# Transposing the merged branch sum in 32x32 blocks on VectorE instead of on TensorE

## The chip, the cores and the metric

The kernel runs on one core of a Trainium2 chip. The metric is the device time of one execution in microseconds (us). The kernel before takes 2072.56 us, the median of 3 runs (2072.18 to 2073.11).

## The reference, cut to what matters

Two layers are computed for 256 tokens of width 2048, all in float32. Three branches (sparse attention, convolution, stick-breaking attention) give gated activations of width 1024. Each is projected to 2048 features, and the three projections are merged by sigmoid gates. One output projection of the merged sum is added to the layer's input:

```python
y_a = (dsa_attention(...) * silu(za)) @ w_a_out
y_b = (conformer_conv(...) * silu(zb)) @ w_b_out
y_c = (stick_breaking_attention(...) * silu(zc)) @ w_c_out
g = sigmoid(gates).reshape(b, s, N_BRANCH, D_MODEL)
merged = g[:, :, 0] * y_a + g[:, :, 1] * y_b + g[:, :, 2] * y_c
return x + merged @ w_out
```

After the second layer comes a last RMSNorm. The change concerns `merged`, between the gates and `w_out`.

## The kernel before, in words

**Units.** Weights are read from HBM in units of 512 KB, 128 partitions x 1024 float32 numbers, and the whole kernel is a row of such units. To multiply float32 numbers accurately, each weight and each activation is split into a high part in the type fp32r and a low remainder. `load_unit` (L181) has SyncE issue the DMA into `raw`; `high` (L202, the copy at L204) has ScalarE (ACT) round it into `wh`; `low` (L206, the subtraction at L208) has VectorE (DVE) form `wl = raw - wh`. `raw` has four buffers, `wh` and `wl` have three each. So `wh` of a unit can be written only when TensorE (PE) is done with the `wh` of the unit three before it, and a `raw` is loaded only when DVE has read the one four before it.

**Products.** `chunk_N` (L277) computes 512 output features for 256 tokens, tokens on the partitions. Each unit is 12 matmuls of 512 columns (`token_products`, L268): four with the activations' high part and `wh`, four with their low part and `wh`, four with their high part and `wl`. PE waits for `wh` at the unit's start and for `wl` at its last third. The activations are the stationary operand, so they have to lie with features on the partitions.

**The merge (L829 to L860).** For each branch b in the order 0, 2, 1 and each quarter j of the 2048 features there is a gate chunk (8 units of `w_in`), a sigmoid by ACT (L849), a projection chunk (4 units of `w_a`, `w_c` or `w_b`), and a product and sum by DVE (L855, or L857 and L858) into `mg`, tokens on the partitions. In the last pass, b = 1, `mg` is complete for quarter j after each projection chunk. It is then turned by `turn(j)` (L819), so that features lie on the partitions, and split into a high and a low part, `mx` (`split_at`, which ends in ACT's copy at L311 and DVE's subtraction at L312).

**The old turn.** It is a generator that `start` puts on a list; `background`, called after each unit's matmuls, resumes it one unit later. Eight PE transposes (L824) of 128x128 write the PSUM tile `mm`; ACT and DVE then split it, at raised priority, straight from PSUM.

**What follows.** Four chunks with `w_out` (L906 to L936) read `mx`, eight units of two 128-feature blocks each. Units 6 and 7 of the first of them are the first to read the last quarter of `mx`, the one that `turn(3)` makes. `residual` (L877) loads the layer's input into a `t4` tile for the add at L889, and for the last layer L871 loads the final norm's weights.

**Order.** The order on each engine and on SyncE's DMA queue is set by a scheduler that ranks instructions by their place in the program, raised where the code says `tc.high_priority()`, and that lets an instruction stand only where its buffer would be free by the scheduler's own reckoning. `t4` is a pool of four buffers of 128 x 1024; it serves the residual tiles, the convolution's norm and the attention branches.

Of the kernel before, what the change touches and what calls it, by code (L numbers as in the profile page):

```python
# [14 lines left out]
P = 128  # L15
S = 256
NT = S // P
# [31 lines left out]
def trunk(ctx: ExitStack, tc: tile.TileContext, x, w_in, w_a, w_b, w_c, w_out,  # L49
          fnw, consts, out):  # L50
    nc = tc.nc
# [25 lines left out]
    ident = cst[:, C_ID:C_ID + P]  # L77
# [15 lines left out]
    def nm(s):  # L93
        uid[0] += 1
        return f"{s}_{uid[0]}"
# [4 lines left out]
    def big():  # L100
        return [slot(), slot()]
# [4 lines left out]
    def parts(n, own=()):  # L106
        own = list(own)
        return own + [slot(F32R).rearrange("p (k w) t -> p k w t", w=2) for _ in range(n // 4 - len(own))]
# [4 lines left out]
    def hi(b, k, n=1, ts=slice(0, S)):  # L113
        return part(b, 0, k, n, ts)

    def lo(b, k, n=1, ts=slice(0, S)):
        return part(b, 1, k, n, ts)

    def split_at(b, k, n, src, ts=slice(0, S)):
        split(hi(b, k, n, ts), lo(b, k, n, ts), src)  # L120

    def mm_tile():
        return mp.tile([P, 1024], F32, tag="mm", name=nm("mm"))
# [4 lines left out]
    def t4():  # L128
        return tp.tile([P, 1024], F32, tag="t4", bufs=4, name=nm("t4"))

    def ev():
        return tp.tile([P, 512], F32, tag="ev", bufs=3, name=nm("ev"))
# [21 lines left out]
    def start(gen):  # L154
        stages.append([gen, 0])

    def finish():
        while stages:
            advance(stages[0])
# [14 lines left out]
    def flush():  # L174
        while waiting:
            for f in waiting.pop(0)[1]:
                f()
# [43 lines left out]
    def chunk_T(w, c0, n, act, nk, t0=0):  # L221
        acc = acc_tile()
        nf = n // P
        nt = S - t0
        ku = min(8, 1024 // n)
        for k0 in range(0, nk, ku):
            wh, wl = unit(w, k0, ku, [(c0, n)])
            for k in range(ku):
                both = act[(k0 + k) // 4][:, (k0 + k) % 4, :, t0:]
                for f in range(nf):  # L230
                    mult(acc[:, f, :2 * nt].rearrange("p (w t) -> p w t", w=2), wh[:, k, f * P:(f + 1) * P],
                         both, k0 + k == 0, False)
            for k in range(ku):
                for f in range(nf):
                    mm = mult(acc[:, f, :nt], wl[:, k, f * P:(f + 1) * P], hi(act, k0 + k)[:, 0, t0:],
                              False, k0 + k == nk - 1)
            background(mm)
        return acc[:, :nf, :2 * nt]
# [7 lines left out]
    def summed(acc):  # L246
        nf = acc.shape[1]
        v = ev()[:, :nf * acc.shape[2] // 2]
        v3 = v.rearrange("p (f t) -> p f t", f=nf)
        total(acc, v3)  # L250
        return v, v3
# [25 lines left out]
    def chunk_N(w, segs, act, nk, ku=2):  # L277
        acc = acc_tile()
        n = sum(c for _, c in segs)
        accs = [acc[:, t, :] for t in range(NT)]  # L280
        for k0 in range(0, nk, ku):
            background(token_products(accs, n, unit(w, k0, ku, segs), act, k0, ku, nk, range(NT)))
        return accs
# [26 lines left out]
    def split(h, l, src):  # L310
        nc.scalar.copy(h, src)  # L311
        nc.vector.tensor_sub(l, src, h.bitcast(F32))  # L312
# [31 lines left out]
    def gate(c0, o, b, w, hx):  # L344
        for k in range(0, KC, 2):
            a, a3 = summed(chunk_T(w, c0 + k * P, 256, hx, KD))
            sg = sigmoid_of(a)
            with tc.high_priority():
                nc.vector.tensor_mul(a3, a3, sg)
                nc.vector.tensor_mul(a3, a3, o[:, k:k + 2, :])  # L350
                split_at(b, k, 2, a3)
# [47 lines left out]
    for layer in range(DEPTH):  # L399
# [153 lines left out]
        for j in range(2):  # L553
            for i in range(2):
# [5 lines left out]
                else:  # L560
                    sg = sigmoid_of(summed(chunk_T(w, O_UG + c0 * P, 256, hx, KD))[0])
                    a = summed(chunk_T(w, O_UA + c0 * P, 256, hx, KD))[1]
# [29 lines left out]
        a = chunk_N(w, [(O_VA, 256), (O_WI, NIH)], hx, KD)  # L592
# [129 lines left out]
        for j in range(2):  # L722
            a = chunk_N(w, [(O_VC + j * 512, 512)], hx, KD)
# [59 lines left out]
        def conv_norm(cv=cv, pr=pr):  # L783
            work = t4()
            red = [work[:, i * S:(i + 1) * S] for i in range(4)]
            sums = red[2:]
            for i in range(2):
                nc.vector.tensor_reduce(red[i], cv[:, i * 4:i * 4 + 4, :].rearrange("p c t -> p t c"), op=ALU.add, axis=AX.X)
            nc.vector.tensor_add(red[0], red[0], red[1])
            yield 3  # L790
            ps = mm_tile()
            nc.tensor.matmul(ps[:, :S], mean_w, red[0], start=True, stop=True)
            for i in range(2):
                cs = cv[:, i * 4:i * 4 + 4, :]
                nc.vector.tensor_sub(cs, cs, heads(ps[:, :S], 4))
                sq = t4()
                nc.scalar.activation(sq.rearrange("p (c t) -> p c t", c=4), cs, AF.Square)
                nc.vector.tensor_reduce(sums[i], sq.rearrange("p (c t) -> p t c", c=4), op=ALU.add, axis=AX.X)
            nc.vector.tensor_add(sums[0], sums[0], sums[1])
            yield 6  # L800
            vs = mm_tile()
            nc.tensor.matmul(vs[:, :S], mean_w, sums[0], start=True, stop=True)
            r = rsqrt_mean(vs[:, :S], 1, t4())
            for i in range(2):
                cs = cv[:, i * 4:i * 4 + 4, :]
                nc.vector.tensor_mul(cs, cs, heads(r, 4))
                sg = t4()
                for c in range(4):
                    cc = i * 4 + c
                    lw, lb = pr[:, P_LW + cc:P_LW + cc + 1], pr[:, P_LB + cc:P_LB + cc + 1]  # L810
                    nc.scalar.activation(sg[:, c * S:(c + 1) * S], cs[:, c, :], AF.Sigmoid, bias=lb, scale=lw)
                    nc.vector.tensor_scalar(cs[:, c, :], cs[:, c, :], lw, lb, op0=ALU.mult, op1=ALU.add)
                nc.vector.tensor_mul(cs, cs, sg.rearrange("p (c t) -> p c t", c=4))
# [3 lines left out]
        mg = [v.rearrange("p a b -> p (a b)").rearrange("p (j t d) -> p j t d", j=2, t=NT) for v in big()]  # L817

        def turn(j, mg=mg):  # L819
            yield 1  # L820
            ps = mm_tile().rearrange("p (k t) -> p k t", t=S)
            for kk in range(4):
                for t in range(NT):
                    nc.tensor.transpose(ps[:, kk, t * P:(t + 1) * P], mg[j // 2][:, j % 2, t, kk * P:(kk + 1) * P],  # L824
                                        ident)
            with tc.high_priority():
                split_at(mx, j * 4, 4, ps)

        for b in (0, 2, 1):  # L829
            if b == 2:  # L830
                finish()
                gc = parts(KC)
                gate(O_ZC, qcT, gc, w, hx)
            if b == 1:
                finish()
                gb = parts(KC)
                gate(O_ZB, cv, gb, w, hx)
                mx = parts(KD)
            gx = ga if b == 0 else gc if b == 2 else gb
            for j in range(4):  # L840
                if b == 2 and j == 1:
                    finish()
                    flush()
                    start(conv_norm())
                g = chunk_N(w, [(O_G + b * D + j * 512, 512)], hx, KD)
                sg = [ev() for _ in range(NT)]
                with tc.high_priority():
                    for t in range(NT):
                        nc.scalar.activation(sg[t], g[t], AF.Sigmoid)  # L849
                y = chunk_N((w_a, w_b, w_c)[b][layer], [(j * 512, 512)], gx, KC)  # L850
                with tc.high_priority():
                    for t in range(NT):
                        dst = mg[j // 2][:, j % 2, t, :]
                        if b == 0:
                            nc.vector.tensor_mul(dst, y[t], sg[t])  # L855
                        else:
                            nc.vector.tensor_mul(sg[t], y[t], sg[t])  # L857
                            nc.vector.tensor_add(dst, dst, sg[t])  # L858
                if b == 1:
                    start(turn(j))  # L860


        last = layer == DEPTH - 1
# [42 lines left out]
        for q in range(3 if last else 4):  # L906
            c0 = q * 512
            tail = residual(c0, 512)
            a = chunk_N(w_out[layer], [(c0, 512)], mx, KD)
# [6 lines left out]
        a = chunk_N(w_out[layer], [(c0, n)], mx, KD, ku=4)  # L916
# [71 lines left out]
```

## Time and profile before

| | |
|---|---|
| median of 3 runs | 2072.56 us (2072.18 to 2073.11) |
| the profiled execution: its own time | 2072.41 us |
| its span, first to last instruction | 2070.6 us |
| outside the span | 1.8 us |
| granted TensorE clock | 0.999 |
| PE busy | 2056.9 us (99%) |
| DVE busy | 1490.4 us (72%) |
| ACT busy | 1067.4 us (52%) |
| DMA | 394.27 MB, mean 190 GB/s |

In the rows that follow, a line number such as L208 is the line of the kernel before. A timeline row gives the start in the span, the time that its merged instructions take, the engine, the line, the operation, output<-input, shapes, how many instructions were merged, and in brackets the engine's idle time before it and what released it. PEld is the load of the stationary operand, which normally runs beside the matmul before it. A grouped row ends in the count, then busy time and mean length of one in ns, then the idle time before the group.

### The profile page before, as it was taken

What the parts mean: (1) busy time and instruction counts of PE and PEld (TensorE: products, weight loads), DVE (VectorE), ACT (ScalarE), POOL (GpSimd) and SP (SyncE); (2) the same over time, 40 slices, a digit from 0 to 9 for tenths busy, and PEclk for the clock granted to TensorE, in tenths of its full rate; (3) what the DMA queues carried; (4) which work ended last, traced back from release to release, by engine and by line L of the source; (5) the groups of instructions that cost most, each with busy time, mean ns of one, the idle gap of its engine ahead of it and who ended that gap; (6) DMA issues with size and microseconds to landing.
All of it is one profiled execution on the core that took longest, in us unless ns stands there. A gap on an engine that the chain in (4) does not pass through costs nothing.

```text
span 2070.6 us, 28574 instructions
## 1 busy us (share of the span) xinstructions
PE 2056.9 (99%) x11056; PEld 1793.6 (87%) x11056; DVE 1490.4 (72%) x2037; ACT 1067.4 (52%) x1309; POOL 0.2 (0%) x4
## 2 busy tenths in 40 slices
PE   9999999999999999999999999999999999999998
PEld 8899888888888888888899998888888888888887
DVE  7678998688776856555576799976887757565555
ACT  6465555466444544444454655554664445444443
POOL 0000000000000000000000000000000000000000
PEclk9999999999999999999999999999999999999999
DMA  7677575665666666666666774756656667666664
GB/s 247 194 220 214 145 204 157 182 179 165 180 190 189 217 209 192 187 190 194 206 191 194 224 204 145 203 152 187 182 162 183 190 194 223 193 192 190 206 196 145
DMA packets 290984, 394.27 MB, mean 190 GB/s; under 512 B 16544, under 2 KB 181536, under 8 KB 290720
## 3 DMA queue, kind: packets, MB, share of 16 engines
q1 hardware_dynamic: 289760, 390.35, 63.6%
q8 instruction: 86, 1.41, 0.3%
q10 hardware_dynamic: 1088, 2.10, 0.3%
q14 instruction: 50, 0.41, 0.1%
HBM read 388.20 MB, written 4.19 MB: 190 GB/s over the span
## 4 chain that ended last, share of the span: by engine, by line
PE 99%; DMA 0%; DVE 0%; ACT 0%; issue 0%; ACTq 0%; SPq 0%
PE acc L218 95%; PE mm L653 1%; PE mm L684 1%; PE mm L373 0%; PE mm L709 0%; PE mm L824 0%; PE mm L772 0%; PE mm L736 0%; PE mm L701 0%; PE mm L758 0%; PE mm L624 0%; PE mm L739 0%; PE mm L774 0%; DMA x<-in_x_dram 0%; PE mm L760 0%; PE mm L763 0%
## 5 line engine op out<-in xcount | busy, mean ns | idle before, releaser
L208 DVE TENSOR_TENSOR wl<-raw,wh 128x1024 fp32r<-128x1024 f32 (+2 forms) x729 | 880.1, 1210 | 474.7 <-ACT wh L204 472.1
L204 ACT CAST wh<-raw 128x1024 fp32r<-128x1024 f32 (+2 forms) x728 | 757.5, 1042 | 848.1 <-PE acc L218 666.5
L218 PE MATMUL acc<-wh,s 128*128 128x512 f32 (+2 forms) x3200 | 775.5, 384 | 0.0
L218 PEld LDWEIGHTS acc<-wh,s 128*128 128x128 f32 x3200 | 587.0, 188 | 114.7
L218 PE MATMUL acc<-s,wh 128*128 128x512 f32 (+2 forms) x2912 | 645.1, 365 | 0.6 <-ACT s L382 0.6
L218 PEld LDWEIGHTS acc<-s,wh 128*128 128x128 f32 x2912 | 492.6, 190 | 62.7 <-ACT s L382 1.0
L218 PE MATMUL acc<-wl,s 128*128 128x512 f32 (+2 forms) x1600 | 417.4, 383 | 0.0
L218 PEld LDWEIGHTS acc<-s,wl 128*128 128x128 f32 x2656 | 356.6, 191 | 18.4
L218 PE MATMUL acc<-s,wl 128*128 128x256 f32 (+1 forms) x2656 | 365.1, 280 | 0.0
L218 PEld LDWEIGHTS acc<-wl,s 128*128 128x128 f32 x1600 | 295.6, 188 | 58.8
L359 DVE SCALAR_TENSOR_TENSOR s<-yT,cst,s 128x256 f32<-128x256 f32 x480 | 217.5, 478 | 0.4
L244 DVE TENSOR_TENSOR ev<-acc,ev 128x512 f32<-128x512 f32 (+2 forms) x60 | 38.4, 640 | 0.0
L857 DVE TENSOR_TENSOR ev<-acc,ev 128x512 f32<-128x512 f32 x32 | 22.0, 688 | 19.3 <-PE acc L218 19.3
L311 ACT CAST s<-ev 128x512 fp32r<-128x512 f32 (+1 forms) x40 | 21.3, 533 | 26.3 <-DVE ev L332 24.5
L325 DVE TENSOR_TENSOR ev<-ev,cst 128x384 f32<-128x384 f32 (+2 forms) x28 | 16.7, 595 | 23.9 <-ACT ev L323 23.8
L243 ACT COPY ev<-acc 128x512 f32<-128x512 f32 (+2 forms) x60 | 32.8, 546 | 0.4 <-PE acc L218 0.4
L312 DVE TENSOR_TENSOR s<-ev,s 128x512 fp32r<-128x512 f32 (+1 forms) x40 | 23.2, 581 | 6.8 <-ACT s L311 6.6
L322 ACT COPY ev<-ev 64x384 f32<-64x384 f32 (+2 forms) x28 | 15.2, 542 | 24.7 <-DVE ev L244 24.3
L849 ACT ACTIVATE ev<-acc 128x512 f32<-128x512 f32 x48 | 26.6, 591 | 0.1
L889 DVE TENSOR_TENSOR t<-acc,t 128x512 f32<-128x512 f32 (+1 forms) x18 | 10.6, 628 | 17.2 <-PE acc L218 17.2
L858 DVE TENSOR_TENSOR s<-s,ev 128x512 f32<-128x512 f32 x32 | 21.9, 685 | 0.0
L341 ACT ACTIVATE ev<-ev 128x512 f32<-128x512 f32 x28 | 17.6, 627 | 0.0
(173 smaller groups left out, 806.4 us busy)
## 6 DMA issues: line engine op xcount, KB each, us to landing
raw<-in_w_in_dram SPq DMA_DIRECT2D x555, 512.0 KB, 3.6
raw<-in_w_out_dram SPq DMA_DIRECT2D x64, 512.0 KB, 4.2
raw<-in_w_a_dram SPq DMA_DIRECT2D x32, 512.0 KB, 3.9
raw<-in_w_c_dram SPq DMA_DIRECT2D x32, 512.0 KB, 3.9
raw<-in_w_b_dram SPq DMA_DIRECT2D x32, 512.0 KB, 3.8
raw<-in_w_in_dram SPq DMA_DIRECT2D x18, 256.0 KB, 3.1
t<-in_x_dram SPq DMA_DIRECT2D x4, 512.0 KB, 6.0
x<-t ACTq DMA_DIRECT2D x4, 512.0 KB, 3.6
```

The lines of the kernel that those rows point to most:

```text
L204: nc.scalar.copy(u[1], u[0])
L208: sub = nc.vector.tensor_sub(u[2], u[0], u[1].bitcast(F32))
L218: newest[0] = nc.tensor.matmul(o, lhsT, rhs, start=start, stop=stop, skip_group_check=True)
L243: nc.scalar.copy(dst, acc[:, :, nt:])
L244: nc.vector.tensor_add(dst, acc[:, :, :nt], dst)
L311: nc.scalar.copy(h, src)
L312: nc.vector.tensor_sub(l, src, h.bitcast(F32))
L359: nc.vector.scalar_tensor_tensor(o, yT[:, c, q:q + S], wq, o, op0=ALU.mult, op1=ALU.add)
L653: nc.tensor.matmul(ps[:, q * S:(q + 1) * S], qi[i][:, hd, :], ki[j][:, 0, :], start=n == 0, stop=n == 2)
L849: nc.scalar.activation(sg[t], g[t], AF.Sigmoid)
L857: nc.vector.tensor_mul(sg[t], y[t], sg[t])
L858: nc.vector.tensor_add(dst, dst, sg[t])
```

## The change

`turn(j)` is no longer a generator that PE steps through later. It is called at once, right after the product and sum of quarter j, and does the transposition on DVE from SBUF to SBUF. The DVE instruction transposes blocks of 32x32, and the 128x128 transposition is put together from such blocks: an instruction reads 32 partitions (32 tokens) and, in each of the four 128-feature groups k, the 32 columns of block b, and writes the four transposed blocks to the 32 partitions of block b. There are 4 (b) x 2 (t) x 4 (a) = 32 such instructions per quarter, 256 in all. From one to the next the input moves on by 32 partitions; the output stays on the same 32 partitions for eight of them. The result `y` is a `t4` tile in SBUF. The split into `mx` reads `y` in place of PSUM, and without raised priority.

```diff
         def turn(j, mg=mg):
-            yield 1
-            ps = mm_tile().rearrange("p (k t) -> p k t", t=S)
-            for kk in range(4):
+
+            y = t4().rearrange("p (k t) -> p k t", t=S)
+            src = [mg[j // 2][:, j % 2, t, :].rearrange("p (k b c) -> p k b c", b=4, c=32) for t in range(NT)]
+            for b in range(4):
                 for t in range(NT):
-                    nc.tensor.transpose(ps[:, kk, t * P:(t + 1) * P], mg[j // 2][:, j % 2, t, kk * P:(kk + 1) * P],
-                                        ident)
-            with tc.high_priority():
-                split_at(mx, j * 4, 4, ps)
+                    for a in range(4):
+                        nc.vector.transpose(y[b * 32:(b + 1) * 32, :, t * P + a * 32:t * P + (a + 1) * 32],
+                                            src[t][a * 32:(a + 1) * 32, :, b, :])
+            split_at(mx, j * 4, 4, y)
...
                 if b == 1:
-                    start(turn(j))
+                    turn(j)
```

In the order of the changed kernel as built, DVE's transposes of a quarter stand in groups of 5, 8, 8, 8 and 3, with one weight subtraction (L208) between one group and the next; the second product and sum of the quarter stands right before the first group. The first group follows the subtraction for unit 3 after the projection chunk's end (counted from 0), and the groups are parted by those for units 4 to 7. After the last group come the subtraction for unit 8 and then L312. On ACT, L311 stands behind the copy (L204) for unit 8. On SyncE's queue, three residual loads of a layer stand directly behind the weight loads for units 7, 8 and 9 of the `w_out` chunks, and a fourth a few units later; in the second layer the 1 MB load of L871 stands behind that of unit 11. In the kernel before, all four residual loads of a layer stood well ahead of the turn, beside the weights of `w_c`, and the load of L871 ahead of the first `w_out` weights.

## The prediction

> **What bounds the kernel now.** I read the page's busy line and the chain that ended last first, then the costliest groups.
>
> ```profile
> PE 2056.9 (99%) x11056; PEld 1793.6 (87%) x11056; DVE 1490.4 (72%) x2037; ACT 1067.4 (52%) x1309; POOL 0.2 (0%) x4
> PE 99%; DMA 0%; DVE 0%; ACT 0%; issue 0%; ACTq 0%; SPq 0%
> L208 DVE TENSOR_TENSOR wl<-raw,wh 128x1024 fp32r<-128x1024 f32 (+2 forms) x729 | 880.1, 1210 | 474.7 <-ACT wh L204 472.1
> ```
>
> PE is the chain: any instruction taken off it is time won, unless PE then waits. DVE idles 474.7 us ahead of its weight subtractions, nearly all of it waiting for ACT's `wh`, which waits for PE to free a buffer: DVE runs at PE's pace, with room in each unit. Next the timeline of PE around the last turn of the first layer.
>
> ```profile
> 948.84 1.98 PE L218 MATMUL acc<-wh,s 128*128 128x512 f32 x8
> 950.65 1.07 PE L218 MATMUL acc<-wl,s 128*128 128x512 f32 x4
> 951.57 1.03 PE L824 MATMUL mm<-cst,s 128*128 128x128 f32 x8
> 952.36 2.07 PE L218 MATMUL acc<-wh,s 128*128 128x512 f32 x8
> 954.27 1.07 PE L218 MATMUL acc<-wl,s 128*128 128x512 f32 x4
> 955.17 1.07 PE L218 MATMUL acc<-wh,s 128*128 128x512 f32 x4
> L824 PE MATMUL mm<-cst,s 128*128 128x128 f32 x64 | 8.3, 272 | 0.0
> ```
>
> **What it removes.** A unit takes 951.57 - 948.84 = 2.73 us (I use 2.72). The eight transposes push the next unit back by 952.36 - 951.57 = 0.79, and that unit takes 955.17 - 952.36 = 2.81, 0.09 more than usual. A turn costs PE 0.88 to 0.89 us; 64 transposes are eight turns: **7.1 us won**. That is all there is to win.
>
> **What it adds to DVE.** 32 instructions per turn, each 128 elements long per partition. No transpose is in this trace, so I bound one by the nearest rows: DVE's short instructions and how closely they follow one another.
>
> ```profile
> 71.19 0.87 DVE L359 SCALAR_TENSOR_TENSOR s<-yT,cst,s 128x256 f32<-128x256 f32 x2
> ...
> 248.76 0.29 DVE L611 MAX8 sm<-sc 64x8 f32<-64x128 f32 x1
> 249.08 0.48 DVE L659 SCALAR_TENSOR_TENSOR sc<-t,sm,sc 128x256 f32<-128x256 f32 x1
> 249.60 0.09 DVE L612 MATCH_VALUE_LOAD sc<-sm,sc 64x8 f32 x1
> 249.70 0.28 DVE L612 MATCH_REPLACE8 sc<-sm,sc 64x128 f32<-64x128 f32 x1
> 250.01 0.49 DVE L359 SCALAR_TENSOR_TENSOR s<-yT,cst,s 128x256 f32<-128x256 f32 x1
> L547 DVE CAST upper_r<-cst 128x128 fp32r<-128x128 f32 x1 | 0.2, 220 | 0.0
> L611 DVE MAX8 sm<-sc 64x8 f32<-64x128 f32 x16 | 4.7, 292 | 0.5
> L633 DVE SCALAR_TENSOR_TENSOR sc<-t,wi,sc 128x128 f32<-128x128 f32 x14 | 4.9, 348 | 0.0
> L208 DVE TENSOR_TENSOR wl<-raw,wh 128x1024 fp32r<-128x1024 f32 x711 | 867.3, 1223 | 474.4 <-ACT wh L204 472.1
> L312 DVE TENSOR_TENSOR s<-ev,s 128x512 fp32r<-128x512 f32 x24 | 16.4, 685 | 0.0
> ```
>
> Two L359 of 0.48 us on all partitions take 0.87 together: the second starts about 0.09 before the first has ended. But L611 and L612 work on partitions 64 to 127, and instructions on partitions from 0 stand around them: 248.76 + 0.29 is followed at 249.08, and 249.70 + 0.28 at 250.01. There the next starts about 0.03 **after** the end. The transposes change their 32 input partitions at every step, so I count them like these: length plus 0.03. For the length, the nearest row is the 292 ns of a one-input pass over 128 elements; below it stands the cast at 220, above it the 348 of a two-input form. A transposed block's first column needs the last of its 32 input columns, so the pipeline may have to fill by 32 elements: at (1223 - 685)/512 = 1.05 ns per element, up to 34 ns more. So a step is 0.32 us at the least row and 0.355 with the fill; I take **0.34**, and 32 are 10.9 us per turn. Both ends of all this stay in the range: 0.13 (the cast, overlapped by 0.09) and 0.45 (twice the elements' time, 292 + 134 + 30 ns, if four-byte data went at half rate).
>
> [...]
>
> **Where the 10.9 us lie.** The rows of DVE and ACT at that place give the rest. I count from 946.12, where PE begins unit 0 of the first `w_out` chunk (the projection chunk's last product ends there, and the first L857 follows at 946.32).
>
> ```profile
> 946.32 0.69 DVE L857 TENSOR_TENSOR ev<-acc,ev 128x512 f32<-128x512 f32 x1 [1.32 <-PE acc L218]
> 946.93 1.22 DVE L208 TENSOR_TENSOR wl<-raw,wh 128x1024 fp32r<-128x1024 f32 x1
> 948.06 0.69 DVE L858 TENSOR_TENSOR s<-s,ev 128x512 f32<-128x512 f32 x1
> 948.66 0.69 DVE L857 TENSOR_TENSOR ev<-acc,ev 128x512 f32<-128x512 f32 x1
> 949.27 1.22 DVE L208 TENSOR_TENSOR wl<-raw,wh 128x1024 fp32r<-128x1024 f32 x1
> 950.40 0.69 DVE L858 TENSOR_TENSOR s<-s,ev 128x512 f32<-128x512 f32 x1
> 945.41 1.05 ACT L204 CAST wh<-raw 128x1024 fp32r<-128x1024 f32 x1 [1.67 <-PE acc L218]
> 952.64 1.02 ACT L311 CAST s<-mm 128x1024 fp32r<-128x1024 f32 x1 [0.73 <-PE mm L824]
> 951.34 1.02 PEld L824 LDWEIGHTS mm<-cst,s 128*128 128x128 f32 x8
> 953.69 1.22 DVE L312 TENSOR_TENSOR s<-mm,s 128x1024 fp32r<-128x1024 f32 x1 [0.52 <-ACT s L311]
> 943.40 1.98 PE L218 MATMUL acc<-wh,s 128*128 128x512 f32 x8
> ```
>
> The L208 at 946.93 follows the copy at 945.41, which PE's last projection unit let go: with three `wh` buffers it is for unit 2. The second L858 starts at 4.28 and is done for the next at 4.9. Then come 32 steps (10.9) and the L208 of units 4 to 7 between them, no longer overlapped: 4 x 1.25 = 5.0. The last step ends at **20.8**.
>
> Quarters 0 to 2 of each layer: nothing reads the result for many units, so only DVE's lag counts. The L208 of unit 7 ends 3 steps before, at 19.8; PE wants that `wl` in the last third of unit 7, at 7 x 2.72 + 1.81 - 0.23 (the load of the stationary operand, 951.34 to 951.57) = 20.6. On ACT the copy for unit 8 lies ahead of L311, and that for unit 9 behind it: L311 waits for 20.8, ends at 21.9, unit 9's copy at 22.9; wanted at 9 x 2.72 - 0.23 = 24.2. So **nothing is lost there**, with 0.8 us to spare: 29 steps stand before unit 7's `wl`, so a step of 0.37 would use it up.
>
> Quarter 3: PE reads it in unit 6, due at 6 x 2.72 = 16.3. L311 ends at 20.8 + 0.05 + 1.02 = 21.9; the first matmul follows 0.05 + 0.23 later, at 22.1, **5.8 late**. The low part: DVE does the L208 of unit 8 (1.14) after 20.8, then L312 from 21.9 to 23.2; PE has done its four high products by 22.1 + 0.9 = 23.0 and goes on at 23.2 + 0.28 = 23.5, 0.4 more. **6.2 us per layer, 12.4 in all.** In the kernel before this wait was nil, as the turn in PSUM was split by 953.69 + 1.22 = 954.9, some 8 us ahead of its reader. PE's own clock: I assume no change over so short a wait.
>
> **Transfers.** Three residual loads of a layer move to beside the weights of units 7 to 9, and the 1 MB load of L871 to unit 11. They are needed at the end of the chunk and later, from 21.8 + 6.2 = 28.
>
> ```profile
> t<-in_x_dram SPq DMA_DIRECT2D x4, 512.0 KB, 6.0
> s<-in_fnw_dram SPq DMA_DIRECT2D x1, 1024.0 KB, 7.5
> raw<-in_w_out_dram SPq DMA_DIRECT2D x64, 512.0 KB, 4.2
> GB/s 247 194 220 214 145 204 157 182 179 165 180 190 189 217 209 192 187 190 194 206 191 194 224 204 145 203 152 187 182 162 183 190 194 223 193 192 190 206 196 145
> DMA packets 290984, 394.27 MB, mean 190 GB/s; under 512 B 16544, under 2 KB 181536, under 8 KB 290720
> ```
>
> Their turns on SyncE's queue come when DVE has read units 3 to 7, from about 5 to 20; the landing takes 6.0 and 7.5, so they are there in time. The weight loads among them are called later too, by DVE's lag, but each is wanted two units after its landing. I cost this at nothing. If that cover were gone, three loads at the mean 190 GB/s would be 8 us of transfer per layer.
>
> **The sum.** 2072.41 (the profiled execution: span 2070.6 and 1.8 around it; the median is 0.15 higher) - 7.1 + 12.4 = **2077.7 us**. With s the step, the wait per layer is 6.2 + 32 (s - 0.34): 0.32 gives 5.6, a sum of 2076.5; 0.355 gives 6.7, a sum of 2078.7.
>
> [...]
>
> **Rivals.** (1) *The steps overlap*, as the L359 pair does: 0.29 - 0.09 = 0.20 each. Then DVE is done by 15.9, and the wait is set by ACT, where L311 stands behind unit 8's copy: that copy starts 2.01 after unit 5 does (945.41 against 943.40 for its like), at 15.6, ends at 16.7; L311 ends at 17.7; PE starts 1.7 late and loses 0.4 more for the low part: 2.1 per layer, 2072.41 - 7.1 + 4.2 = 2069.5. This ends not slower. For it speaks the pair; against it, the rows at 248.76 and 249.70. It wins over the old kernel from a step below 0.26.
> (2) *Half rate*: 0.45. The last quarter waits 6.2 + 32 x 0.11 = 9.7, and in the six other turns unit 7's `wl` is late by 29 x (0.45 - 0.37) = 2.3: 2072.41 - 7.1 + 19.4 + 13.8 = 2098.5. Nothing in the trace speaks for or against it.
> [...]
> (3) *The transfers collide*: late weights cost up to 8 us per layer, 2086 to 2094. The slices of the span reach 247 GB/s, so there is room over 190.
> That the change doesn't do what it says is excluded: in the built order the 64 PE transposes are gone.
>
> **Chances.** About 0.2% (4.1 us) is what a measurement of this kernel can tell from no change. Steps of 0.32 to 0.37, my forecast: 0.52, 2076.5 to 2079.6. Steps of 0.26 to 0.32, where gain and wait nearly cancel, 2072 to 2076.5: 0.15. Rival 1: 0.14. Steps between 0.37 and 0.45 and rival 2: 0.14. Rival 3: 0.05. Faster by over 0.2% would need 2068.4, beyond the floor of rival 1: 0.03 for an error in it. Within 0.2%: 0.11 + 0.15 = 0.26. Slower: 0.71. The range leaves out part of rival 1 and the far part of rival 2: 2070 to 2092.
>
> **What would show it.** Right: no PE wait in quarters 0 to 2; one of some 6 us at unit 6 of the first `w_out` chunk in each layer, put down to ACT's L311; steps of 0.32 to 0.36 start to start; DVE busy up by about 80 us. Wrong: steps that overlap; PE waiting for `wl` in every turn; PE waiting for a DMA.

## The result and the profile after

The changed kernel takes **2077.40 us** (median of 16 runs, 2075.28 to 2078.98); the kernel before, on the same chips, 2072.78 (16 runs, 2071.65 to 2074.53). The ratio is 1.0021, 95% interval 1.0014 to 1.0028: **slower by 0.21%**. The profiled execution took 2075.32 us with a span of 2073.5, at the short end of its runs; where it differs from most of them is part of what follows.

The page of the changed kernel first (all its lines behind L826 stand one below those of before: L858 is the old L857, L890 the old L889).

```profile
PE 2053.6 (99%) x10992; PEld 1788.8 (86%) x10992; DVE 1563.8 (75%) x2293; ACT 1065.4 (51%) x1309; POOL 0.2 (0%) x4
...
PE 98%; DVE 1%; ACT 0%; issue 0%; DMA 0%; ACTq 0%; SPq 0%
...
L208 DVE TENSOR_TENSOR wl<-raw,wh 128x1024 fp32r<-128x1024 f32 (+2 forms) x729 | 878.3, 1208 | 405.6 <-ACT wh L204 401.7
...
L826 DVE STREAM_TRANSPOSE t<-s 32x128 f32<-32x128 f32 x256 | 77.5, 303 | 4.1
```

PE is busy 3.3 us less, with 64 instructions fewer, and the span is 2.9 us longer. DVE has 73.4 us more work, and its idle time ahead of the weight subtractions shrank from 474.7 to 405.6: VectorE found nearly all of its new time in waits that cost nothing. The chain of waits still runs through PE, but 1% of it is DVE now. PE's waits, by their releasers:

```profile
PE acc L218 <- ACT s L311: 5.9, 2, 2.9
PE mm L373 <- DMA x<-in_x_dram: 4.4, 1, 4.4
...
PE acc L218 <- ACT wh L204: 0.5, 2, 0.2
```

The second row is the start of the program and is there before too. The other two are new, twice each: once per layer, and nowhere in quarters 0 to 2. Here is the place in the first layer on VectorE and ScalarE:

```profile
943.43 0.69 DVE L858 TENSOR_TENSOR ev<-acc,ev 128x512 f32<-128x512 f32 x1 [1.31 <-PE acc L218]
...
948.11 1.56 DVE L826 STREAM_TRANSPOSE t<-s 32x128 f32<-32x128 f32 x5
949.61 1.17 DVE L208 TENSOR_TENSOR wl<-raw,wh 128x1024 fp32r<-128x1024 f32 x1
950.81 2.51 DVE L826 STREAM_TRANSPOSE t<-s 32x128 f32<-32x128 f32 x8
953.35 1.23 DVE L208 TENSOR_TENSOR wl<-raw,wh 128x1024 fp32r<-128x1024 f32 x1
...
962.24 0.94 DVE L826 STREAM_TRANSPOSE t<-s 32x128 f32<-32x128 f32 x3
963.21 1.04 ACT L311 CAST s<-t 128x1024 fp32r<-128x1024 f32 x1 [3.32 <-DVE t L826]
```

Eight steps take 2.51 to 2.53 us, so a step is 0.317 us: 303 ns and a gap of 14 (31 at one step of the 32, the fifth; where input and output partitions change together it is 14 too). The last block is written at 963.18, L311 follows at once. And TensorE:

```profile
958.64 1.07 PE L218 MATMUL acc<-wl,s 128*128 128x512 f32 x4
959.94 1.42 PE L218 MATMUL acc<-wh,s 128*128 128x512 f32 x5 [0.24 <-ACT wh L204]
964.31 2.59 PE L218 MATMUL acc<-wh,s 128*128 128x512 f32 x10 [2.95 <-ACT s L311]
966.74 1.09 PE L218 MATMUL acc<-wl,s 128*128 128x512 f32 x4
```

Unit 5 is done at 959.55, which is when unit 6 was due. The five products at 959.94 aren't unit 6: they belong to the *next* chunk's first unit, which the built order sets ahead of the waiting product (two more of them stand in the ten at 964.31). PE waits 0.24 + 2.95 = 3.2 us, and unit 6 starts 964.31 - 959.55 = 4.8 late.

The second layer waits as long, but look at what follows its wait. First TensorE's timeline, then the windows, where the column behind POOL's is the granted clock:

```profile
1991.07 4.63 PE L218 MATMUL acc<-wh,s 128*128 128x512 f32 x10 [2.92 <-ACT s L311]
1995.50 1.75 PE L218 MATMUL acc<-wl,s 128*128 128x512 f32 x4
```

```profile
1988.00:1992.00 4.00, 1.08 (x3) 0.83 (x3) 3.91 (x6) 2.01 (x2) 0.00 (x0) 0.76 0.49 132
1992.00:1996.00 4.00, 4.00 (x11) 3.04 (x10) 0.32 (x1) 0.73 (x3) 0.00 (x0) 0.50 1.00 376
1996.00:2000.00 4.00, 4.00 (x17) 3.29 (x16) 1.22 (x1) 1.68 (x2) 0.00 (x0) 0.88 0.35 117
```

The same ten products take 4.63 us instead of 2.59: the granted clock is **0.50** for some 6 us after the wait. In the first layer of this execution it stayed at 1.00.

What each layer lost can be read between two landmarks on VectorE that both kernels have: the first product with the gate of the last quarter (L857, now L858), and the residual sum of the second `w_out` chunk (L889, now L890). Before:

```profile
991.74 1.29 DVE L889 TENSOR_TENSOR t<-acc,t 128x512 f32<-128x512 f32 x2 [1.31 <-PE acc L218]
...
1972.86 0.69 DVE L857 TENSOR_TENSOR ev<-acc,ev 128x512 f32<-128x512 f32 x1 [1.31 <-PE acc L218]
...
2017.27 1.29 DVE L889 TENSOR_TENSOR t<-acc,t 128x512 f32<-128x512 f32 x2 [1.31 <-PE acc L218]
```

After:

```profile
991.77 1.29 DVE L890 TENSOR_TENSOR t<-acc,t 128x512 f32<-128x512 f32 x2 [1.31 <-PE acc L218]
...
1970.18 0.69 DVE L858 TENSOR_TENSOR ev<-acc,ev 128x512 f32<-128x512 f32 x1 [1.00 <-PE acc L218]
...
2020.18 1.29 DVE L890 TENSOR_TENSOR t<-acc,t 128x512 f32<-128x512 f32 x2 [1.32 <-PE acc L218]
```

At the first landmark the changed kernel is 946.32 - 943.43 = 2.9 us ahead: three turns won. At the second it is level (991.77 against 991.74): with the fourth turn's 0.9 also won, the wait cost 3.8. In the second layer it gains 2.7 up to the landmark (from 0.0 behind to 2.7 ahead) and is 2.9 behind at 2020.18: with the fourth turn's 0.9, this wait cost 6.5. 2.9 + 0.9 + 2.7 + 0.9 - 3.8 - 6.5 = -2.9, the whole difference of the spans.

So the theory to test has three parts. **W**: TensorE wins 0.89 us per turn, in quarters 0 to 2 at no price, and the last turn of each layer costs a wait, because it has no later work ahead of its reader. **H**: the steps don't overlap since each changes its group of 32 partitions. **C**: the wait makes the clock fall, and that costs about as much as three turns win. Rivals stand with each run. All ratios below are to the kernel before on the same chip.

### The profile page after: what moved, and what is told of

Read it like the earlier page. It is cut to its first block, busy times and chain, and to the rows that moved or that the text cites. A ratio compares the mean times of both kernels' runs of the same rounds, so it can differ in the third digit from the quotient of the medians.

```text
span 2073.5 us, 28705 instructions
## 1 busy us (share of the span) xinstructions
PE 2053.6 (99%) x10992; PEld 1788.8 (86%) x10992; DVE 1563.8 (75%) x2293; ACT 1065.4 (51%) x1309; POOL 0.2 (0%) x4
## 4 chain that ended last, share of the span: by engine, by line
PE 98%; DVE 1%; ACT 0%; issue 0%; DMA 0%; ACTq 0%; SPq 0%
PE acc L218 94%; DVE t L826 1%; PE mm L653 1%; PE mm L684 1%; DVE wl L208 0%; PE mm L373 0%; PE mm L709 0%; PE mm L772 0%; PE mm L736 0%; PE mm L701 0%; PE mm L758 0%; PE mm L624 0%; PE mm L739 0%; PE mm L774 0%; DMA x<-in_x_dram 0%
## 5 line engine op out<-in xcount | busy, mean ns | idle before, releaser
L204 ACT CAST wh<-raw 128x1024 fp32r<-128x1024 f32 (+2 forms) x728 | 756.7, 1042 | 833.4 <-PE acc L218 645.7
L208 DVE TENSOR_TENSOR wl<-raw,wh 128x1024 fp32r<-128x1024 f32 (+2 forms) x729 | 878.3, 1208 | 405.6 <-ACT wh L204 401.7
L826 DVE STREAM_TRANSPOSE t<-s 32x128 f32<-32x128 f32 x256 | 77.5, 303 | 4.1
L858 DVE TENSOR_TENSOR ev<-acc,ev 128x512 f32<-128x512 f32 x32 | 22.0, 687 | 19.0 <-PE acc L218 19.0
L311 ACT CAST s<-ev 128x512 fp32r<-128x512 f32 (+1 forms) x40 | 21.3, 533 | 26.0 <-DVE ev L332 24.5
L312 DVE TENSOR_TENSOR s<-ev,s 128x512 fp32r<-128x512 f32 (+1 forms) x40 | 23.2, 580 | 6.8 <-ACT s L311 6.6
L322 ACT COPY ev<-ev 64x384 f32<-64x384 f32 (+2 forms) x28 | 15.2, 542 | 24.5 <-DVE ev L244 24.1
L890 DVE TENSOR_TENSOR t<-acc,t 128x512 f32<-128x512 f32 (+1 forms) x18 | 10.6, 627 | 17.4 <-PE acc L218 17.4
L311 ACT CAST s<-t 128x1024 fp32r<-128x1024 f32 x8 | 8.4, 1049 | 26.5 <-DVE t L826 26.5
```

Of the source, the lines that this page charges most:

```text
L204: nc.scalar.copy(u[1], u[0])
L208: sub = nc.vector.tensor_sub(u[2], u[0], u[1].bitcast(F32))
L826: nc.vector.transpose(y[b * 32:(b + 1) * 32, :, t * P + a * 32:t * P + (a + 1) * 32], src[t][a * 32:(a + 1) * 32, :, b, :])
```

## Experiments: which turn costs

**The last turn back on TensorE.** `turn_pe` is the old `turn`.

```diff
 if b == 1:
-    turn(j)
+    if j == 3:
+        start(turn_pe(j))
+    else:
+        turn(j)
```

> The turn of the last quarter goes back to TensorE and PSUM; those of quarters 0 to 2 stay on VectorE. Theory W (the change costs time only where the first w_out chunk waits for the last quarter, and in a lower clock right after that wait): six turns' worth of TensorE time is won and nothing lost, 2072.8 - 6 x 0.89 = 2067.5 us. Rival V (VectorE's load delays the whole merge): three quarters of the loss stay, about 2076.

Measured: **2067.58 us** (11 runs, 2066.37 to 2068.42), ratio 0.9976 [0.9967, 0.9985]. No wait of PE is left in this stage, and the clock over the span of the profiled execution is 0.999, as before. Six turns on VectorE win 2072.42 - 2067.58 = 4.8 us where 6 x 0.89 = 5.3 were to be won; the ratio's interval, 3.1 to 6.8 us, holds both.

**Only the last turn on VectorE**, the opposite half.

```diff
-    turn(j)
+    if j < 3:
+        start(turn_pe(j))
+    else:
+        turn(j)
```

> Only the turn of quarter 3 goes through VectorE; those of quarters 0 to 2 stay on TensorE. Theory W (the whole loss hangs on the last turn of each layer, the other six are pure gain): the changed kernel's 2077.4 plus the six turns that come back to TensorE, 6 x 0.89 = 5.3: 2082.7 us, and in the trace one wait per layer of about 3.2 us at unit 6 put down to the cast of L311 (two lines later here). Rival V (each turn on VectorE costs something like the same, by delayed weight halves): the changed kernel's loss of 4.6 comes from eight turns, two are left, so about 2072.8 + 1.2 = 2074.

Measured: **2081.80 us** (5 runs, 2081.49 to 2082.82), ratio 1.0043 [1.0031, 1.0056]. V is out. The wait is that of the changed kernel to the tenth:

```profile
PE acc L218 <- ACT s L311: 5.9, 2, 2.9
```

The halves add up: 4.8 won and 8.7 lost (2081.80 - 2073.11, the kernel before on that chip) make 3.9 lost, with 4.6 measured for both together; the interval of the changed kernel's ratio reaches from 2.9 to 5.8.

**The last turn read later.** All turns on VectorE; units 6 and 7 of the first `w_out` chunk, which read it, are moved behind the first two units of the second chunk. It holds two sums open at a time: `open_chunk` opens one, `steps` runs units into it.

```diff
...
+if q == 0:
+    tail, a = open_chunk(0)
+    steps(a, 0, range(0, 12, 2))
+    tail1, a1 = open_chunk(512)
+    steps(a1, 512, (0, 2))
+    steps(a, 0, (12, 14))
+elif q == 1:
+    tail, a = tail1, a1
+    steps(a, 512, range(4, KD, 2))
...
```

> All turns on VectorE as in the changed kernel, but units 6 and 7 of the first w_out chunk, the first readers of the last quarter, come after the first two units of the second chunk: 5.4 us of other work ahead of them. Theory W: the wait is covered, and with it the lower clock goes: 2072.8 - 7.1 = 2065.7 us, up to 0.5 more for the low part. Rival V (VectorE's load delays the merge itself): still about 2077.

Measured: **2065.09 us** (5 runs, 2064.49 to 2066.62), ratio 0.9967 [0.9954, 0.9979], clock 0.999. This beats both kernels: 7.3 us won, the whole of the eight turns. VectorE's work is the same, 256 instructions in 77.5 us, and L311 comes no sooner. Only its reader moved. ScalarE's row and then TensorE's:

```profile
963.28 1.05 ACT L311 CAST s<-t 128x1024 fp32r<-128x1024 f32 x1 [3.32 <-DVE t L826]
```

```profile
965.05 1.98 PE L218 MATMUL acc<-wh,s 128*128 128x512 f32 x8
966.86 1.07 PE L218 MATMUL acc<-wl,s 128*128 128x512 f32 x4
967.77 1.98 PE L218 MATMUL acc<-wh,s 128*128 128x512 f32 x8
```

The cast ends at 964.33. Unit 6, the first to read it, starts at 965.05, unit 7 at 967.77, and no row of PE shows idle time. The two units put in between are just enough: the high part is there 0.7 us ahead, and the low part (L312, done at 965.64) some 0.1 us ahead of the weight load for it, due at 965.05 + 4 x 0.227 - 0.23 = 965.73.

**Twice the steps in quarters 0 to 2**, on top of the last kernel: how much room has VectorE there? The blocks of each output group `b` are written twice, with the same values.

```diff
-for b in range(4):
+for b in (0, 1, 2, 3) if j == 3 else (0, 0, 1, 1, 2, 2, 3, 3):
```

> The kernel that reads the last quarter later (2065.1 us), with each pass over an output group made twice in quarters 0 to 2, so that 64 blocks' steps instead of 32 lie on VectorE in six turns; the second pass writes the same values again. Theory W (VectorE hides 32 steps only because unit 7's low weights are just in time, with some 0.8 us to spare): with 0.317 us per step and 1.25 per weight subtraction, 8 steps and one subtraction take 3.79 us per unit of 2.72, so the lag grows by 1.07 per unit; unit 11's low weights come at 4.9 + 61 x 0.317 + 8 x 1.25 = 34.2 where TensorE wants them at 31.5: 2.7 us late per turn, 16 in six turns: about 2081 us, with TensorE waiting for wl in units 7 to 11. Rival R (VectorE idles 474 us in all, so 48 more instructions' time per turn finds room): stays at 2065.

Measured: **2104.2 us** (4 runs, 2102.94 to 2105.46), ratio 1.015 [1.0137, 1.0164]. R is out, but W's price was 2.4 times too small: 39 us over its base, not 16. TensorE waits for low weights as expected, and this row alone has 24.1 of the 39 us:

```profile
PE acc L218 <- DVE wl L208: 24.1, 28, 0.9
```

What I had left out is that the lag isn't made good before the next turn. Two successive quarters on VectorE:

```profile
845.68 0.69 DVE L858 TENSOR_TENSOR ev<-acc,ev 128x512 f32<-128x512 f32 x1 [1.32 <-PE acc L218]
...
884.75 0.68 DVE L858 TENSOR_TENSOR ev<-acc,ev 128x512 f32<-128x512 f32 x1
```

The second has no wait at all: VectorE is busy from one to the other, 39.07 us, while TensorE's quarter is 12 units of 2.72, 32.6. The difference of 6.4, six times, is 38.6. VectorE has become the bound of these quarters. It also says how much room the change itself leaves. VectorE's quarter has twelve subtractions of 1.25, four passes of some 0.65 and an L312 of 1.2, 18.8 us in sum, and 32 steps of 0.317 make it 28.9 of 32.6. So a step could take up to an estimated (32.6 - 18.8) / 32 = 0.43 us before the quarter as a whole overflows.

## Experiments: what sets a step

**Two steps per group of partitions.** The token half `t` runs innermost, so that every second step keeps its input partitions (it always keeps its output partitions within a `b`).

```diff
 for b in range(4):
-    for t in range(NT):
-        for a in range(4):
+    for a in range(4):
+        for t in range(NT):
```

> The changed kernel with the loops of the turn in the order b, a, t in place of b, t, a: every second transpose reads and writes the same 32 partitions as the one before. Theory H (a change of the 32 input partitions holds the next instruction back): 16 of 32 steps are about 0.1 us shorter, the last quarter is ready 1.5 us sooner, the wait falls to under 2 us and no longer lowers the clock: about 2072.8 - 7.1 + 2 x 2 = 2069.7 us. Rival (the gap between transposes is the same whatever they read): 2077.4 us.

Measured: **2070.53 us** (11 runs, 2069.43 to 2072.76), ratio 0.9991 [0.9983, 1.0], the same 256 instructions and now not slower than before. Eight steps:

```profile
951.33 2.14 DVE L826 STREAM_TRANSPOSE t<-s 32x128 f32<-32x128 f32 x8
```

From end to next start the trace has -63 to -70 ns where both groups of partitions stay, and +13 to 14 where the input ones change. 0.27 us per step instead of 0.317 brings the cast 1.4 us forward, and the wait from 2.95 to 1.59:

```profile
963.60 2.56 PE L218 MATMUL acc<-wh,s 128*128 128x512 f32 x10 [1.59 <-ACT s L311]
```

The time falls by 6.9 us where two waits shrink by 2.7 together. The rest fits the clock: in both layers of this execution it stays at 1.00 behind the wait, and the measured terms without a fall, 2072.42 - 7.1 + 2 x (3.8 - 1.4), give 2070.1. Only this one execution has a trace, so whether the others had a fall isn't shown.

**The output partitions changing at each step, the input ones every fourth.**

```diff
-for b in range(4):
+for a in range(4):
     for t in range(NT):
-        for a in range(4):
+        for b in range(4):
```

> The same 256 block transposes with the loops turned: the 32 input partitions stay the same for four steps while the output partitions change at each. Theory H (a change of the output's group of partitions holds an instruction back as a change of the input's does): a step stays between 0.317 (as in the changed kernel, where only the input's group changes inside a run) and 0.335, eight steps take 2.5 to 2.7 us, and the time is 2077 to 2079 us, with the wait at unit 6 and the half clock as before. Rival I (only the input's group matters): three steps of four overlap by 0.07 to 0.08 as they do where both stay, eight steps take about 1.95 us, TensorE waits about 1.5 us per layer without a half clock, and the time is about 2069.5 us.

Measured: **2077.32 us** (11 runs, 2075.06 to 2078.61), ratio 1.002 [1.0011, 1.0029], eight steps in 2.51 us, end to next start 14 ns. H holds: a change of the output's group keeps a step back as one of the input's does, as the three orders of the loops show (14, 14, and 14 beside -63 to -70 ns).

This run also answers why most executions of the changed kernel are longer than the profiled one. Its waits are the same (2.93 and 2.92 us), its profiled time, 2077.32, is that of a median run, and here the clock fell in **both** layers, to a mean of 0.996 over the span. The changed kernel's own runs say the same: the clock is 0.997 in the three shortest, 2075.28 to 2076.20 us, the profiled one among them, and 0.996 in the other thirteen. The windows of the first layer, then of the second:

```profile
964.00:968.00 4.00, 2.88 (x7) 2.30 (x8) 2.36 (x2) 2.53 (x3) 0.00 (x0) 0.57 0.73 228
968.00:972.00 4.00, 4.00 (x19) 3.31 (x18) 1.22 (x1) 1.24 (x2) 0.00 (x0) 1.00 0.47 165
...
1992.00:1996.00 4.00, 2.88 (x7) 2.31 (x8) 2.36 (x2) 2.53 (x3) 0.00 (x0) 0.50 0.86 285
1996.00:2000.00 4.00, 4.00 (x14) 3.11 (x13) 0.68 (x1) 1.04 (x1) 0.00 (x0) 0.65 0.78 305
```

## Experiments: what the clock costs

To take the clock apart from the wait, TensorE is given useless products (512 columns, into a PSUM tile that nobody reads) ahead of unit 6; `tc.issue_after` puts them behind unit 5's last product. The useful products then stand in one order for all counts, and all wait for the same cast.

```diff
+if fill and k0 == 12:
+    junk = mm_tile()
+    with tc.issue_after(newest[0].ins):
+        for i in range(fill):
+            nc.tensor.matmul(junk[:, i % 2 * 512:i % 2 * 512 + 512], hi(act, 0)[:, 0, :P],
+                             act[0][:, 0, :, :], start=True, stop=True, skip_group_check=True)
```

**18 of them.**

> The changed kernel, with 18 matmuls of 512 columns whose result nobody reads (4.1 us of TensorE work) put where TensorE waits for the last quarter, ahead of unit 6 of the first w_out chunk of each layer. They take the place of the few matmuls of the next chunk that stand there now. Theory W: unit 6 starts when the last quarter is ready, about 4.8 us late, plus 0.3 for its low part, and the clock stays whole: 2072.8 - 7.1 + 2 x 5.1 = 2075.9 us, granted clock 0.999, matmuls 0.23 us apart behind the wait. Rival C (what is lost beside the wait has nothing to do with the clock): the same loss on top, about 2080 us.

Measured: **2076.34 us** (11 runs, 2075.41 to 2077.04), ratio 1.0019 [1.001, 1.0028].

```profile
1988.85 4.24 PE L286 MATMUL mm<-s 128*128 128x512 f32 x18
1993.62 2.51 PE L218 MATMUL acc<-wh,s 128*128 128x512 f32 x8 [0.53 <-ACT s L317]
```

The five products that the changed kernel pulls forward are not pulled forward here, and 4.24 us of useless work stand in their place in each layer; yet the time is no longer than the changed kernel's. The clock is 1.00 in the second layer's windows from 1988 to 2000, and the eight products behind the wait take 2.51 us there and 2.52 in the first layer.

**8 of them.** The only difference to the last kernel is less work for TensorE.

> As in the filled kernel (18 useless products of 512 columns ahead of unit 6, 2076.3 us), with 8 of them instead of 18: TensorE's useful work stands in the same order and comes at the same moments, only 2.3 us less of useless work stands in the wait, so that TensorE is idle there for about 2.9 us, as in the changed kernel, instead of 0.53. Theory C (an idle time of about 3 us lets the granted clock fall to half for some 6 us, which costs 2.9 us each time): slower than with 18, 2079 us with one fall and 2082 with a fall in each layer, though TensorE is given less to do. Rival N (the clock plays no part, the wait ends with the cast in both): the same 2076.3 us.

Measured: 2078.78 us (9 runs, 2076.44 to 2081.16), ratio 1.0025 [1.0015, 1.0035]. That lies above 18's 1.0019, as C wants, but the intervals overlap and the chips were different ones. So three counts were run on one chip.

> 16 useless products of 512 columns ahead of unit 6, on the same chip as 12 and 8 of them: TensorE's useful work comes in the same order and waits for the same cast; the idle time before it is 0.53 + 2 x 0.23, about 1.0 us. Theory C (idle time of about 3 us lets the clock fall): no fall, as with 18, a ratio of 1.0019 to the kernel before, about 2076.5 us. Rival N: the same.

> 12 useless products: idle for 0.53 + 6 x 0.23, about 1.9 us. Theory C: the waits of 1.6 us in the kernel whose steps overlap were not followed by a lower clock, so here mostly none, 2076.5 us, or with a fall in some layers up to 2079. Rival N (the clock plays no part): 2076.5.

> 8 useless products again, now on the same chip as 16 and 12, since on another chip the interval left it open: idle for about 2.8 us. Theory C: at least 2 us above the kernel with 16 on this chip, with windows of half clock behind the wait. Rival N: the same time as with 16.

| useless products | idle ahead of unit 6 | median (runs) | range | clock over the span, all runs | ratio |
|---|---|---|---|---|---|
| 16 | 0.98 us | 2076.33 (11) | 2075.48 to 2077.22 | 0.999 | 1.0018 [1.0009, 1.0027] |
| 12 | 1.89 us | 2077.91 (9) | 2076.47 to 2078.90 | 0.998 to 0.999 | 1.0023 [1.0013, 1.0033] |
| 8 | 2.79 us | 2078.41 (11) | 2076.68 to 2080.33 | 0.997 to 0.998 | 1.0026 [1.0017, 1.0035] |

The less TensorE had to do, the longer the kernel took, by 2.1 us from the first row to the last. The wait ends 4.76 to 4.77 us behind the start of the first useless product in both layers of all three traces. The intervals of the ratios still overlap, and the clock over the span has the program's end in it, where TensorE idles at half clock (for the last 4.9 us of the changed kernel's trace, 5.2 of that of the kernel before), so that 0.998 alone doesn't tell one short fall from none. What carries the verdict is the trace. With 12, TensorE's timeline in the first layer, then in the second:

```profile
964.16 3.35 PE L218 MATMUL acc<-wh,s 128*128 128x512 f32 x8 [1.89 <-ACT s L317]
967.30 1.86 PE L218 MATMUL acc<-wl,s 128*128 128x512 f32 x4
...
1994.01 2.51 PE L218 MATMUL acc<-wh,s 128*128 128x512 f32 x8 [1.88 <-ACT s L317]
1996.36 1.08 PE L218 MATMUL acc<-wl,s 128*128 128x512 f32 x4
```

The same twelve products behind the same wait take (967.30 + 1.86) - 964.16 = 5.0 us in one layer and 3.4 in the other. The granted clock in the windows from 964 and from 1992 is 0.70 in the one and 1.00 in the other:

```profile
964.00:968.00 4.00, 3.72 (x10) 2.74 (x11) 1.42 (x2) 2.01 (x4) 0.00 (x0) 0.70 0.70 231
...
1992.00:1996.00 4.00, 2.00 (x8) 1.26 (x8) 3.21 (x5) 2.53 (x3) 0.00 (x0) 1.00 0.71 192
```

C holds, and with a chance in it: after an idle time of 0.5 or 1.0 us none of 11 runs each shows a lower clock over the span; after 1.9 one layer of the two in the trace fell; after 2.8 to 2.95 some layers fell and some didn't, for different lengths of time. My expectation for 12, mostly no fall, was too low by 1.4 us.

**When it falls.** The traces hold the changes of the granted clock, and they show what the chance is. Within one execution all changes lie on one grid of 3.413 us: the stretches at half clock around these waits last 3.413 or 6.827 us (6.827 in the changed kernel's second layer), and the stretches at full clock are whole multiples of it as well (1979.730 and 71.680 us in the changed kernel's trace and 2054.823 in that of the kernel before, which are 580, 21 and 602 times 3.4133). In these traces it isn't the length of a wait that parts the falls from the rest, but how much of a window of this grid TensorE was idle. Cut at the grid, with all idle time of a window added up:

| execution, layer | idle time in successive windows with the wait | clock behind |
|---|---|---|
| changed kernel, first | 1.56 and 1.62 us | 1.00 |
| changed kernel, second | 1.97 and 0.96 us | 0.50 for two windows |
| 12 useless products, first | 2.01 us | 0.50 for one window |
| 12 useless products, second | 0.84 and 1.16 us | 1.00 |

In all 13 traces, from the clock's first record some 10 us into the span to the program's end, each window with 1.97 us of idle time or more was followed by half clock, and none with 1.62 us or less was, unless the clock was at half already. No window lies between the two. A second window at half clock followed where the first one was itself idle for 0.96 us (the changed kernel's second layer) or 1.12 us (the second layer with the output partitions changing at each step), and none where it was idle for 0.58 us or less. So of two waits of 1.9 us the one that lay within a window lowered the clock, and the one that an edge parted didn't; the changed kernel's first layer escaped in the same way. Where the grid stands differs from execution to execution (the clock's first record lies at 10.38 us in the changed kernel's trace, at 10.59 in that of the kernel before), and no run here sets it.

## Why the prediction was right, point by point

- **7.1 us won on TensorE**: right. With the wait taken away, 7.3 are won (2072.42 - 2065.09 on one chip), and PE has 64 instructions fewer.
- **A step of 0.34 us**: it measures 0.317, at the least row's bound (0.32). The block's fill that I added isn't to be seen: 303 ns is 11 above the one-input pass of 292, where the fill was up to 34. That the steps don't overlap was right (of the two rows named for it, the one at 249.70 follows an instruction on its own partitions, and the rows at 249.08 and 250.01 show the gap), and so rival 1 failed by its premise; half of it, in the order with `t` innermost, gave 2070.5 us, close to rival 1's 2069.5. Rival 2 is out with a step far below 0.45.
- **Last block 20.8 us after unit 0's start**: 963.18 - 943.23 (unit 0's start) = 20.0.
- **Nothing lost in quarters 0 to 2**: right, by the trace, by the kernel with the last turn on TensorE and by the one that reads later. The room named there was one unit's only; for a quarter as a whole the doubled kernel shows where it ends.
- **Transfers cost nothing**: right, no row of PE waits for a transfer here.
- **6.2 us of waiting per layer, 12.4 in all**: **this step failed**: it is 2.4 us too long per layer. Unit 6 is 4.8 late, not 5.8 (0.7 of the difference is the step, 32 x 0.023). Of those 4.8, TensorE fills 5 x 0.227 = 1.1 with products of the next chunk, and two more cover the 0.4 that the low part was to cost (with 18 useless products in their place, unit 6's eight products take 2.51 instead of 1.98). I took the order of the units in the source for that of the instructions; the built order of the changed kernel shows these products ahead of the waiting one. What is left is a wait of 3.2 us and a cost of 3.8 per layer: the 7.2 us from 959.55 to 966.74 hold fifteen products, 15 x 0.227 = 3.4, the wait and another 0.6.
- **"PE's own clock: I assume no change over so short a wait"**: **this failed too**, with the other sign. The fall of the clock costs up to 6.5 - 3.8 = 2.7 us per layer in the traced execution. The sum by the measured terms is 2072.41 - 7.1 + 2 x 3.8 = 2072.9 with no fall, 2075.6 with one of this size, and 2078.3 with two; the profiled execution is the second, and most runs lie between the second and the third.

That 2077.7 stands so near to 2077.4 is luck: a wait taken 2 x 2.4 = 4.8 us too long stood in for a fall of the clock that was put at nothing. The sign rested on the last turn alone and was right; without the fall of the clock the measured terms give 2072.9, no change that can be measured.

## What to carry to other kernels

Work moved from the bound engine to one with room is won only where its reader stands far enough behind; look at the last piece of each stage, which has no later work to hide it, and move its reader before you judge the engine (2077.4 became 2065.1 that way). Read who waits from the order of instructions as built, since it may have filled part of the wait already. And count a wait of TensorE like those of 1.89 to 2.95 us here, of which some were followed by a clock of 0.50 and some weren't, as the wait and a possible fall of its clock with it: the waits alone ate the gain (2072.9 by the measured terms), and the clock made the loss.

## What the runs showed of the hardware

- A block transpose of four-byte data on 32 partitions by 128 elements takes 303 ns. The next starts 63 to 70 ns before its end, and takes some 260 ns itself, if both groups of partitions stay; it starts 13 to 14 ns after the end if one of them changes or both do (31 to 32 at one step of the 32).
- In these traces the granted clock changed only on a grid of 3.413 us that runs through an execution. It fell to 0.50 for a window behind each window with 1.97 to 3.41 us of idle time on TensorE, and behind none with up to 1.62 us. So waits of 1.89 to 2.95 us had a fall in some layers and none in others, by where the grid cut them, and those of 0.53 and 0.98 us had none.
